# Four reciprocal norms reach all partitions through a row in DRAM instead of products with the identity

## The chip, the cores and the metric

The kernel runs as one program on one core of a Trainium2 chip. The metric is the device time of one execution in microseconds (us); the figures below are a median of three runs and one profiled execution. TensorE is called PE here, its weight loads PEld, VectorE DVE, ScalarE ACT, GpSimd POOL and the DMA queue of SyncE SP. A profile line number such as L289 is a line of the kernel file before the change.

## The reference

A trunk of two layers over 512 tokens of width 1024, all in float32. Each layer has a mixing part and a SwiGLU feed-forward part (FFN), and each part first divides every token by the root mean square of its 1024 features.

```python
def rms_norm(x, g):
    x32 = x.astype(jnp.float32)
    y = x32 * lax.rsqrt(jnp.mean(x32 * x32, axis=-1, keepdims=True) + EPS)
    return (y * g).astype(x.dtype)

def reference(x, ...):
    h = x
    for layer in range(DEPTH):                      # 2
        hn = rms_norm(h, mixer_norm_g[layer])
        if layer % 2 == 0:                          # retention and pooling, joined
            h = h + retention_pool_mixer(hn, positions, ...)
        else:                                       # pointwise + GLU, causal conv of width 31,
            h = h + conformer_conv(hn, ...)         # LayerNorm, swish, pointwise
        h = h + swiglu(rms_norm(h, ffn_norm_g[layer]), w_gate[layer], w_up[layer], w_down[layer])
    return rms_norm(h, final_norm_g)
```

So there are five such norms: one ahead of the mixer of layer 0, one ahead of each FFN, one ahead of the convolution part of layer 1, and the final one. The first four are touched by the change.

## The kernel before, in words

The residual `X` lies in SBUF feature-major: 128 features on the partitions, 8 tiles of features, 512 tokens along the free dimension. Products run in float32 accuracy as three products of split operands: a high part, rounded, and a low part that holds the rest (`mm3`: high by high, high by low, low by high). Weights come in chunks of 1 MB into a ring of two raw buffers (`wr`), and are split into a high part `wh` (ACT cast) and a low part `wl`. For most chunks `wl` is a DVE subtraction (L186); for the second and third chunk of each FFN and most chunks of the convolution part ACT writes minus the high part and a DMA issued by POOL adds the raw values to it (L178, L1353). A raw buffer is free for the next load only when that DMA has landed.

The norm is not applied to the operand: `X` times its gain goes into the products, and the reciprocal root `r` of each token multiplies their results. Since tokens lie along the free dimension of those results, `r` is needed as a tile with the same 512 values on every partition. The steps of one norm are:

- squares of `X` are summed over the feature tiles into `acc` [128 x 512];
- `token_sums` (L281) multiplies each block of 128 tokens of `acc`, as the stationary operand, by a column of ones. That gives a PSUM tile [128 x 4] with token `128 t + p` at partition `p`, column `t`;
- `inv_rms` (L296) scales it and `rsqrt` (L264 to L271) takes the reciprocal root with eleven small DVE instructions;
- `spread` (L284) takes each of the four columns, broadcast along the free dimension, as the stationary operand of a product with the identity, which puts the 128 values on every partition; ACT copies the PSUM tile to SBUF (L293).

Where it is done:

- In the mixer, `rtok` (the result of `rsqrt`) is also used per token as a column, for `v` (L614) and for the gate (L651). Its spread form multiplies the tables `cosr` and `sinr` of the rotary positions (L497, L498) and the channels of the pooling groups (L534), out of which ACT and DVE make the split operands `yh` and `yl` of the product `ps_p`.
- In each FFN the first three chunks of gate and up weights are ordinary products (`ps_gu`); the spread stands inside the second of these (between its k = 4 and k = 5, L987), and the DVE instruction L884 in `hidden` reads it first. The further 19 chunks go through `cycle`, a scheme with seven half products in place of eight.
- In the convolution part the spread stands inside the second projection `proj(1)` (L1381); `gated` (L1191) reads it for each of the eight projections. Between those DVE instructions DVE works through 31 taps of the depthwise convolution for each of three feature tiles (`some_taps`, L1329); PE does the other five tiles (`conv_tile`). After the taps of two tiles, `pivot_sum` adds them into `acc` (L1301), whose token sums PE forms.

Order: in the FFNs the order on PE, DVE and ACT is the program's (`manual_schedule`); SP and POOL are placed by a planner, which lists instructions by its own costs. In the convolution part SP is in program order too. In the mixer only the first block is in program order; from `rb = spread(rtok, "rms")` (L496) on, the planner places everything. In the convolution part a chunk's raw load is one `start_load()`, and `split_rest` is a generator whose two steps each cast half a chunk; its second step is run inside `gated`, after the sigmoid:

```python
                rest = split_rest()
                next(rest)
                proj(4)
                some_taps(1)
                gated(3, pss[3], FULL, two_taps, rest)
                to_rows(3, FULL)
                start_load()
                some_taps(9)
```

Of the kernel before, what the change touches and what calls it, by code (L numbers as in the profile page):

```python
# [10 lines left out]
F32 = mybir.dt.float32  # L11
# [3 lines left out]
ALU = mybir.AluOpType  # L15
PSUM = bass.MemoryType.PSUM

P = 128
D = 1024
S = 512  # L20
KT = D // P
NT = S // P
# [7 lines left out]
EPS = 1e-6  # L30
# [3 lines left out]
FULL = slice(0, S)  # L34
# [49 lines left out]
def trunk(ctx: ExitStack, tc: tile.TileContext, a: dict):  # L84
    nc = tc.nc
# [7 lines left out]
    wk = ctx.enter_context(tc.tile_pool(name="wk", bufs=2))  # L93
    pmm = ctx.enter_context(tc.tile_pool(name="pmm", bufs=3, space=PSUM))
    paux = ctx.enter_context(tc.tile_pool(name="paux", bufs=2, space=PSUM))

    vec = const.tile([P, NVEC], F32, name="vec")
    con = const.tile([P, NCON], F32, name="con")
# [13 lines left out]
    ones = C("ones")  # L112
# [90 lines left out]
    def feature_major(ps, wh, wl, xh, xl, cols=FULL, between={}, ks=range(KT)):  # L203

        for k in ks:
            if k in between:
                between[k]()
            for i in range(2):
                c = slice(i * P, (i + 1) * P)
                mm3(ps[:, i, cols], wh[:, k, c], wl[:, k, c], xh[k][:, cols], xl[k][:, cols], k == 0, k == KT - 1)  # L210
# [27 lines left out]
    xgh = [None] * KT  # L238
    xgl = [None] * KT
# [32 lines left out]
            between()  # L272
        return y

    def token_sums(acc, cols=FULL):

        ps = paux.tile([P, S], F32, tag="aux", name="ps_ms")
        n = (cols.stop - cols.start) // P
        for t in range(n):
            at = cols.start + t * P  # L280
            nc.tensor.matmul(ps[:, t:t + 1], lhsT=acc[:, at:at + P], rhs=ones, start=True, stop=True)  # L281
        return ps[:, :n]

    def spread(v, name, out=None):  # L284

        n = v.shape[1]
        ps = paux.tile([P, S], F32, tag="aux", name=f"ps_{name}")
        for t in range(n):
            nc.tensor.matmul(ps[:, t * P:(t + 1) * P], lhsT=v[:, t:t + 1].to_broadcast([P, P]),  # L289
                             rhs=ident, start=True, stop=True)  # L290
        if out is None:
            out = wk.tile([P, n * P], F32, tag=f"bc_{name}", name=f"bc_{name}", bufs=1)
        nc.scalar.copy(out, ps[:, :n * P])  # L293
        return out

    def inv_rms(acc):  # L296
        v = sm.tile([P, NT], F32, tag="ms", name="ms")
        nc.vector.tensor_scalar(v, token_sums(acc), 0.5 / D, 0.5 * EPS, ALU.mult, ALU.add)
        return rsqrt(v, NT, "a4")

    def new_acc():
# [26 lines left out]
    def mixer():  # L328
        with ExitStack() as m:
# [9 lines left out]
            acc = new_acc()  # L339
# [64 lines left out]
            with tc.manual_schedule(engines={mybir.EngineType.PE, mybir.EngineType.DVE, mybir.EngineType.Activation,  # L404
# [68 lines left out]
                ps = token_sums(acc)  # L473
# [4 lines left out]
                v = sm.tile([P, NT], F32, tag="ms", name="ms")  # L478
# [11 lines left out]
            for src in range(2):  # L490
                ps_, ts_ = slice(src * HP, (src + 1) * HP), slice(src * HS, (src + 1) * HS)
                for dst in range(2):
                    pd = slice(dst * HP, (dst + 1) * HP)
                    nc.scalar.activation(cosr[pd, ts_], kq[ps_], AF.Sin)
                    nc.scalar.activation(sinr[pd, ts_], ang[ps_], AF.Sin, scale=2.0 * dst - 1.0)
            rb = spread(rtok, "rms")  # L496
            nc.vector.tensor_tensor(cosr, cosr, rb, ALU.mult)  # L497
            nc.vector.tensor_tensor(sinr, sinr, rb, ALU.mult)  # L498

# [157 lines left out]
            acc = new_acc()  # L657
# [39 lines left out]
    def ffn_in(layer, acc, gain, fx, fl, fh, fe, ff):  # L697
# [275 lines left out]
        scaled(2)  # L973
        scaled(3)
        combined_lo(1)
        r = inv_rms(acc)
        load_gu(f0)
        plain_hi(f0)
        load = split_load()
# [4 lines left out]
        for _ in load:  # L984
            pass
        ps.append(pair("ps_gu1"))
        feature_major(ps[1], *w, xgh, xgl, between={5: lambda: row.update(rb=spread(r, "rms"))})  # L987
        add_up(f0)
        combined_lo(2)
        combined(3)  # L990
# [175 lines left out]
    def conv(acc):  # L1166
        with ExitStack() as m:
# [167 lines left out]
            def note(name, f, *args):  # L1335
                row[name] = f(*args)
# [22 lines left out]
            def proj(j, between={}):  # L1359
                pss[j] = pair(f"ps_pw{j}")  # L1360
                feature_major(pss[j], *chunk("w_pw1", j, 0), xgh, xgl, between=between)
# [10 lines left out]
            with tc.manual_schedule(engines={mybir.EngineType.PE, mybir.EngineType.DVE, mybir.EngineType.Activation,  # L1372
# [5 lines left out]
                proj(0, {7: lambda: note("r", inv_rms, acc)})  # L1378
                for _ in split_rest():
                    pass  # L1380
                proj(1, {2: lambda: note("rb", spread, row["r"], "rms")})  # L1381
                rb = row["rb"]
                start_load()
                gated(0, pss[0], FULL)
                some_taps(9)
# [220 lines left out]
```

## Time and profile before

| | |
|---|---|
| median of 3 runs | 1048.3 us (1048.09 to 1048.49) |
| profiled execution: its own time, its span | 1047.62 us, 1045.8 us |
| granted clock of TensorE | 0.998 |
| busy share of the span: PE, PEld, DVE, ACT, POOL | 99%, 87%, 81%, 49%, 3% |
| DMA traffic | 121.63 MB, mean 116 GB/s |
| products of `spread` for the four norms (L289, `ps_rms`) | 32 rows of PE, median 275 ns |
| copies of the four spread tiles (L293, `bc_rms`) | 4, median 568 ns |
| token sums (L281) on `acc` | 48 rows of PE, median 250 ns |

A busy row of PE overlaps the next one, since products are pipelined; what a product costs is better read from the distance between the starts of two rows. In a timeline row the columns are start, duration, engine, line, operation, tiles and shape; the bracket at the end gives the idle time of that engine just before the row and what ended it. In a row of waits, the numbers are the total, how many, and the longest. In a row of windows, they are the length of the window, then busy time and number of instructions of PE, PEld, DVE, ACT and POOL, then the granted clock, the DMA share and GB/s. Rows of DMA issues end with the size of one transfer and its median time from issue to landing.

### The profile page before, as it was taken

The numbers are of one execution on the slowest core, as the hardware profiler recorded it, in microseconds if no ns is written. First come the engines' busy times: TensorE is split into PE (matmuls) and PEld (weight loads), VectorE is DVE, ScalarE is ACT, GpSimd is POOL, SyncE is SP. The second block draws the span as 40 slices with busy tenths as digits, with TensorE's granted clock in tenths as the row PEclk, the third lists the DMA queues.
The fourth block names the chain that finished last, engine by engine and source line by source line (L and its number), as shares of the span: only waits on it lengthen the run. The fifth ranks groups of instructions, "written<-read, shape, count | busy, mean of one in ns | idle before, by whom it ended". The sixth has DMA issues, their size and how long they took to land.

```text
span 1045.8 us, 16517 instructions
## 1 busy us (share of the span) xinstructions
PE 1035.9 (99%) x6705; PEld 907.9 (87%) x6705; DVE 850.5 (81%) x1297; ACT 515.9 (49%) x881; POOL 32.5 (3%) x33
## 2 busy tenths in 40 slices
PE   9999999999999999999999999999999999999997
PEld 7878888899999999998888665988999999999987
DVE  7888735889988889997779797859999888899855
ACT  8543134765454545543444325656654455445434
POOL 0000000100000000001121100000000000000000
PEclk9999999999999999999999999999999999999999
DMA  8322122643323322333248996146233332323122
GB/s 300 132 81 81 41 81 88 184 136 116 111 92 104 119 91 92 122 118 125 81 94 188 222 189 149 59 139 174 72 121 121 102 121 76 112 96 122 41 81 81
DMA packets 38108, 121.63 MB, mean 116 GB/s; under 512 B 4112, under 2 KB 13328, under 8 KB 29584
## 3 DMA queue, kind: packets, MB, share of 16 engines
q1 hardware_dynamic: 34432, 107.99, 32.4%
q0 software_dynamic: 3456, 12.58, 6.3%
q8 instruction: 52, 0.85, 0.3%
q14 instruction: 24, 0.20, 0.1%
q10 hardware_dynamic: 144, 0.00, 0.0%
HBM read 100.36 MB, written 2.10 MB: 98 GB/s over the span
## 4 chain that ended last, share of the span: by engine, by line
PE 88%; DVE 6%; ACT 2%; DMA 2%; issue 1%; DVEq 0%; ACTq 0%
PE ps_x L854 19%; PE ps_y L854 10%; PE ps_dn L199 7%; PE ps_dn L200 7%; PE ps_dn L201 7%; PE ps_z L854 5%; PE ps_c L1229 2%; PE ps_gu L201 2%; PE ps_gu L199 2%; PE ps_gu L200 2%; PE ps_pw L199 2%; PE ps_pw L201 2%; PE ps_pw L200 2%; DMA wr<-in_w_pw 2%; PE ps_wo L201 1%; PE ps_wo L200 1%
## 5 line engine op out<-in xcount | busy, mean ns | idle before, releaser
L854 PE MATMUL ps_x<-th,w 128*128 128x256 f32 x608 | 115.9, 276 | 0.3 <-ACT sn L929 0.3
L765 DVE TENSOR_TENSOR wg<-wg 128x512 f32<-128x512 f32 x152 | 105.3, 693 | 5.1
L774 ACT CAST w<-wg 128x512 fp32r<-128x512 f32 x152 | 82.9, 618 | 37.3 <-PE ps_y L854 36.0
L854 PEld LDWEIGHTS ps_x<-th,w 128*128 128x128 f32 x608 | 97.2, 188 | 0.5 <-ACT sn L929 0.5
L779 DVE TENSOR_TENSOR w<-wg,w 128x2048 fp32r<-128x2048 f32 x38 | 87.1, 2291 | 10.5 <-ACT w L774 10.1
L854 PE MATMUL ps_x<-tl,w 128*128 128x256 f32 x304 | 83.9, 276 | 0.0
L311 DVE TENSOR_TENSOR X<-X,ps_dn 128x1024 f32<-128x1024 f32 x46 | 56.0, 1218 | 18.6 <-PE ps_dn L201 18.6
L183 ACT CAST w<-wr 128x2048 fp32r<-128x2048 f32 (+2 forms) x22 | 34.8, 1599 | 56.6 <-PE ps_g L573 21.8
L199 PE MATMUL ps_dn<-hh,dh0d 128*128 128x512 f32 x152 | 59.4, 391 | 0.0
L200 PE MATMUL ps_dn<-hl,dh0d 128*128 128x512 f32 x152 | 59.4, 391 | 0.0
L201 PE MATMUL ps_dn<-hh,dl0d 128*128 128x512 f32 x152 | 59.2, 390 | 0.1
L854 PE MATMUL ps_y<-th,w 128*128 128x256 f32 x304 | 57.9, 276 | 0.0
L854 PE MATMUL ps_y<-xgh,w 128*128 128x256 f32 x304 | 57.9, 276 | 0.0
L854 PEld LDWEIGHTS ps_x<-tl,w 128*128 128x128 f32 x304 | 57.1, 188 | 0.0
L939 ACT COPY sn<-ps_x 128x256 f32<-128x256 f32 x38 | 14.2, 374 | 85.9 <-PE ps_x L854 85.9
L200 PE MATMUL ps_dn<-hl,dh1d 128*128 128x512 f32 x144 | 56.2, 391 | 0.0
L199 PE MATMUL ps_dn<-hh,dh1d 128*128 128x512 f32 x144 | 56.2, 391 | 0.0
L201 PE MATMUL ps_dn<-hh,dl1d 128*128 128x512 f32 x144 | 56.0, 389 | 0.0
L854 PE MATMUL ps_x<-xgh,w 128*128 128x256 f32 x288 | 55.2, 277 | 0.0
L878 DVE TENSOR_TENSOR hl<-act,hh 128x512 fp32r<-128x512 f32 x44 | 30.5, 692 | 26.3 <-ACT hh L877 26.1
L877 ACT CAST hh<-act 128x512 fp32r<-128x512 f32 x44 | 27.3, 621 | 48.0 <-DVE act L872 44.0
L199 PE MATMUL ps_pw<-xgh,w 128*128 128x512 f32 x128 | 50.3, 393 | 0.0
(346 smaller groups left out, 3098.9 us busy)
## 6 DMA issues: line engine op xcount, KB each, us to landing
wg<-in_w_gu SPq DMA_DIRECT2D x38, 1024.0 KB, 4.9
dr<-in_w_dn SPq DMA_DIRECT2D x64, 256.0 KB, 2.9
w<-wr POOLq DMA_DIRECT2D x24, 512.0 KB, 5.3
wr<-in_w_pw SPq DMA_DIRECT2D x10, 1024.0 KB, 5.1
wr<-in_w_gu SPq DMA_DIRECT2D x6, 1024.0 KB, 4.9
dr<-in_w_dn SPq DMA_DIRECT2D x32, 192.0 KB, 2.5
wr<-in_w_o SPq DMA_DIRECT2D x4, 1024.0 KB, 4.9
R<-u SPq DMA_DIRECT2D x12, 270.0 KB, 14.6
```

The lines of the kernel that those rows point to most:

```text
L183: nc.scalar.copy(wh[:, s], raw[:, s])
L199: nc.tensor.matmul(out, lhsT=wh, rhs=xh, start=start, stop=False)
L200: nc.tensor.matmul(out, lhsT=wh, rhs=xl, start=False, stop=False)
L201: nc.tensor.matmul(out, lhsT=wl, rhs=xh, start=False, stop=stop)
L311: nc.vector.tensor_tensor(xx, xx, ps, sign)
L765: nc.vector.tensor_tensor(o, o, i, ALU.add)
L774: nc.scalar.copy(block(sums[f][0], *SUMS[i]), block(raw_g[f], *SUMS[i]))
L779: nc.vector.tensor_tensor(l, raw_g[f], h.bitcast(F32), ALU.subtract)
L854: nc.tensor.matmul(out, lhsT=u[:, k, :], rhs=v, start=first and k == 0 and n == 0, stop=k == 3 and n == 2, skip_group_check=True)
L877: nc.scalar.copy(hh[f], s)
L878: return lambda: nc.vector.tensor_tensor(hl[f], s, hh[f].bitcast(F32), ALU.subtract)
L1229: nc.tensor.matmul(ps[32 * i:32 * i + 32, :n], lhsT=dgs[j][:, i, g, :], rhs=Rs[j][:, i, 4 * g + cols.start:4 * g + cols.stop], start=g == ...
```

## The change

`spread` stays for the three uses inside the convolution part's LayerNorm. For the four norms `spread_row` takes its place: one DMA on SP writes the 512 values into a row of 2 KB in DRAM, a second DMA on SP reads that row back to all 128 partitions (256 KB in SBUF). For the two FFNs and the convolution part the token sums are formed with tokens taken in steps of four (`by=NT`), so that partition `p` holds the tokens `4p` to `4p + 3`, four neighbours of 16 bytes in the row. In the mixer `rtok` keeps its layout, as `v` and the gate use it; there the write puts single values 512 bytes apart. The result tile has the same name `bc_rms`. In the FFNs the call now stands directly behind `inv_rms`, in the convolution part ahead of `proj(1)`, in the mixer at the place of the old call.

```diff
+    dr = ctx.enter_context(tc.tile_pool(name="dr", bufs=2, space=bass.MemoryType.DRAM))
...
-    def token_sums(acc, cols=FULL):
+    def token_sums(acc, cols=FULL, by=1):
         ps = paux.tile([P, S], F32, tag="aux", name="ps_ms")
         n = (cols.stop - cols.start) // P
+        if by > 1:
+            for t in range(n):
+                nc.tensor.matmul(ps[:, t:t + 1], lhsT=acc.rearrange("p (q t) -> p t q", t=n)[:, t, :], rhs=ones,
+                                 start=True, stop=True)
+            return ps[:, :n]
...
+    def spread_row(v, name, tokens="(p t) -> p t"):
+        row = dr.tile([S], F32, tag="row", name=f"row_{name}")
+        out = wk.tile([P, S], F32, tag=f"bc_{name}", name=f"bc_{name}", bufs=1)
+        nc.sync.dma_start(row.rearrange(tokens, t=NT), v)
+        nc.sync.dma_start(out, row.partition_broadcast(P))
+        return out
+
     def inv_rms(acc):
         v = sm.tile([P, NT], F32, tag="ms", name="ms")
-        nc.vector.tensor_scalar(v, token_sums(acc), 0.5 / D, 0.5 * EPS, ALU.mult, ALU.add)
+        nc.vector.tensor_scalar(v, token_sums(acc, by=NT), 0.5 / D, 0.5 * EPS, ALU.mult, ALU.add)
         return rsqrt(v, NT, "a4")
...   (mixer)
-            rb = spread(rtok, "rms")
+            rb = spread_row(rtok, "rms", "(t p) -> p t")
...   (FFN)
-        r = inv_rms(acc)
+        row["rb"] = spread_row(inv_rms(acc), "rms")
         load_gu(f0)
         plain_hi(f0)
         load = split_load()
...
-        feature_major(ps[1], *w, xgh, xgl, between={5: lambda: row.update(rb=spread(r, "rms"))})
+        feature_major(ps[1], *w, xgh, xgl)
...   (convolution part)
-                proj(1, {2: lambda: note("rb", spread, row["r"], "rms")})
-                rb = row["rb"]
+                rb = spread_row(row["r"], "rms")
+                proj(1)
                 start_load()
```

## The prediction

> **What bounds the kernel now.** I read the totals first, then what the weight loads of TensorE (PEld) waited for, then the four places where the rows are spread, each as a timeline.
>
> ```profile
> span 1045.8 us, 16517 instructions
> PE 1035.9 (99%) x6705; PEld 907.9 (87%) x6705; DVE 850.5 (81%) x1297; ACT 515.9 (49%) x881; POOL 32.5 (3%) x33
> PEld ps_p L199 <- ACT yh L231: 1.3, 3, 0.5
> ...
> PEld ps_gu L201 <- DMA w<-wr: 0.7, 2, 0.4
> L289 PE MATMUL ps_rms<-con,rs_y x32: 271/275/275, 31.3 to 715.5; 128*128 128x128 f32 x32
> L281 PEld LDWEIGHTS ps_ms<-con,acc x48: 186/192/192, 24.2 to 707.6; 128*128 128x128 f32 x48
> ```
>
> PE is busy for 1035.9 of 1045.8 us, so whatever PE no longer does could come back one for one, unless PE then stands at one of its waits. Two of them are quoted (total, number, longest): in the mixer PE waits for yh, which ACT casts from pooled channels made on DVE; in the two FFN layers, once each, for the low part of a weight chunk, w<-wr, which POOL's accumulating DMA finishes. A third, in the convolution layer, comes below. The removed work is 32 rows on PE, 8 for each of the four norms (an f32 product shows as two).
>
> **Price of one spread on PE.** FFN of layer 0:
>
> ```profile
> 200.25 0.39 PE L200 MATMUL ps_gu<-xgl,w 128*128 128x512 f32 x1
> 200.47 0.39 PE L201 MATMUL ps_gu<-xgh,w 128*128 128x512 f32 x1
> ...
> 201.82 0.39 PE L200 MATMUL ps_gu<-xgl,w 128*128 128x512 f32 x1
> ```
>
> Products of 512 columns start 0.22 us apart (200.25, 200.47). Two of them after the one at 200.47 the row at 201.82 should have started at 200.92; it started 0.90 us later. One spread costs PE 0.9 us, four 3.6 us. That is the most that this part can give. The four ACT copies that go save nothing of their own: ACT is busy for half of the span, and where the copy does end a wait (the convolution layer) it is counted there.
>
> **Mixer: -0.9.**
>
> ```profile
> 29.89 0.16 DVE L271 SCALAR_TENSOR_TENSOR rs_y<-rs_t,rs_y 128x4 f32<-128x4 f32 x1
> 34.24 0.33 SPq L147 DMA_DIRECT2D wr<-in_w_u  x1
> 40.47 0.69 DVE L497 TENSOR_TENSOR cosr<-cosr,bc_rms 128x512 f32<-128x512 f32 x1 [3.88 <-ACT cosr L494]
> ```
>
> rtok is ready at 30.05 (29.89 + 0.16). DVE uses the spread row only at 40.47, where it waited for the cosines. A row that lands before that costs nothing: the two transfers have 10.4 us of cover, and the mixer's write, the slowest of the four, is priced among the rivals. Without that cover DVE, and through yh PE, would be late one for one. SP issues its next load at 34.24; if that has to pass the second transfer it shifts by at most the time of one write. PE's 0.9 us can come back here. What speaks against it is the wait for yh (1.3 us of weight loads, three times): DVE's chain from 40.47 does not move, so PE would reach yh sooner. But the order of PE's products there is the planner's, and others can stand in front. Bounds: 0 if those waits take it all, -0.9 if they take nothing; I take -0.9, since the waits are short and the products between them many.
>
> **The two FFN layers: 0 on PE, +0.2 each by traffic.**
>
> ```profile
> 181.09 0.33 SPq L720 DMA_DIRECT2D wg<-in_w_gu  x1
> 194.02 0.33 SPq L147 DMA_DIRECT2D wr<-in_w_gu  x1
> 197.99 0.16 DVE L271 SCALAR_TENSOR_TENSOR rs_y<-rs_t,rs_y 128x4 f32<-128x4 f32 x1
> 199.10 1.05 ACT L176 CAST w<-wr 128x1024 fp32r<-128x1024 f32 x1 [0.26 <-DMA wr<-in_w_gu]
> 201.53 0.86 POOL L178 DMA_DIRECT2D w<-wr  x1 [11.78 <-ACT w L177]
> w<-wr POOLq DMA_DIRECT2D x1, 512.0 KB, 4.6
> 206.16 0.49 PE L201 MATMUL ps_gu<-xgh,w 128*128 128x512 f32 x1
> 206.75 1.22 DVE L884 TENSOR_TENSOR gu<-ps_gu,bc_rms 128x1024 f32<-128x1024 f32 x1
> 209.59 3.80 SPq L720 DMA_DIRECT2D wg<-in_w_gu  x2
> 719.91 0.39 PE L200 MATMUL ps_gu<-xgl,w 128*128 128x512 f32 x1
> 720.29 0.50 PE L201 MATMUL ps_gu<-xgh,w 128*128 128x512 f32 x1
> ```
>
> The third chunk of weights is loaded by SP at 194.02, cast by ACT at 199.10 (it waited for that load), and its low part is accumulated by POOL at 201.53, landing 4.6 us later at 206.13. PE reads it at 206.16, 0.03 later. In layer 1 the same product shows the wait plainly: it starts at 720.29, 0.38 after the one at 719.91 instead of 0.22. This chain of SP, ACT and POOL starts before the spread and contains no product of it, so with 0.9 us less work PE stands 0.9 us longer at the same product. Gain 0, twice; a gain is excluded because PE already waits. The new token sums have the same 8 loads; a slower load would be hidden in this 0.9 us too. The row is needed at 206.75: r ends at 198.15 and two transfers have 8.6 us. Behind them on SP comes a load that is not issued before 209.59, so nothing else is late there. What can be lost is traffic: the 256 KB read runs from about 200.5 to 203.5, and w<-wr moves its 512 KB from about 202.4 on. Half a microsecond is the upper bound (dr below takes 0.9 longer for 256 KB than the shortest transfer; two that share take half of that from each other), 0 the lower; I take +0.2 each, nearer to 0, as the two overlap for one microsecond of three.
>
> **Convolution layer: +1.8.** This is where the change decides.
>
> ```profile
> 532.45 0.16 DVE L271 SCALAR_TENSOR_TENSOR rs_y<-rs_t,rs_y 128x4 f32<-128x4 f32 x1
> 536.44 1.23 DVE L1191 TENSOR_TENSOR gu<-ps_pw,bc_rms 128x1024 f32<-128x1024 f32 x1 [3.79 <-ACT bc_rms L293]
> 541.61 14.48 SPq L147 DMA_DIRECT2D wr<-in_w_pw  x2
> 536.00:538.00 2.00, 2.00 (x11) 1.63 (x10) 1.23 (x1) 1.97 (x3) 0.86 (x1) 1.00 1.10 207
> 539.27:578.76 39.49, 39.49 (x176) 32.69 (x175) 39.03 (x59) 17.04 (x18) 5.25 (x7) 1.00 0.80 187
> 570.61 0.86 POOL L1353 DMA_DIRECT2D w<-wr  x1 [1.98 <-ACT w L1352]
> w<-wr POOLq DMA_DIRECT2D x1, 512.0 KB, 9.2
> 579.91 0.34 SPq L147 DMA_DIRECT2D wr<-in_w_pw  x1
> 591.98 1.04 ACT L1351 CAST w<-wr 128x1024 fp32r<-128x1024 f32 x1 [10.97 <-DMA wr<-in_w_pw]
> 594.76 0.75 DVE L1196 SCALAR_TENSOR_TENSOR u<-gu,vec,act 128x512 f32<-128x512 f32 x1 [5.12 <-ACT act L1192]
> 605.45 1.05 PE L281 MATMUL ps_ms<-con,acc 128*128 128x1 f32 x8 [0.29 <-DVE acc L1301]
> ```
>
> r is there at 532.61. Before, the products and the copy brought it to DVE at 536.44, and DVE stood idle for 3.79 us. From then on DVE is full: 39.03 of 39.49 us up to 578.76. Out of that queue comes gated(3), behind whose sigmoid ACT casts half a chunk, which POOL accumulates at 570.61 (9.2 us to landing, 579.81); this frees the buffer for SP's load at 579.91, ACT's cast waits for that load until 591.98 with the sigmoid of gated(5) behind it, DVE waits 5.12 us for the sigmoid, does 14 more taps, and PE waits for the sum at 605.45. So a late row goes through DVE, ACT, POOL, SP, a DMA, ACT and DVE to PE without a gap larger than the 0.46 us that DVE had free. PE's own 0.9 us is lost at 605.45, where it waits already.
>
> How late is the row? Both transfers are on SP, the second behind the completion of the first. Nothing else is held up on SP: its next load is issued at 541.61, for a buffer that is not free before. No row shows a small write to DRAM; the nearest are these:
>
> ```profile
> DMA to landing us min/median/max: 2.0/2.5/2.7
> dr<-in_w_dn SPq DMA_DIRECT2D x64, 256.0 KB, 2.9
> vg<-in_vec ACTq DMA_DIRECT2D x1, 4.0 KB, 3.1
> R<-u SPq DMA_DIRECT2D x4, 142.0 KB, 3.9
> ```
>
> The first is out<-o, the only writes to DRAM in the trace (256 KB): 2.0 at least, 2.5 in the median. vg, 128 short runs, took 3.1. For the write of 128 runs of 16 B I take 2.25, bounds 2.0 and 3.1. For the 256 KB read, dr took 2.9 for the same size; the DMA engines are full at that time (share 1.10 in 536 to 538, POOL's accumulations), so 3.2, bounds 2.5 (the median of out<-o) and 3.9 (R<-u, which moves half as much in 512 runs). With 0.1 us ahead of each issue: 532.61 + 2.25 + 3.2 + 0.2 = 538.26, which is 1.8 us after 536.44. Bounds: 537.3 (+0.9) and 539.8 (+3.4). I do not subtract DVE's free 0.46 us: the read will hold up POOL's accumulations about as much.
>
> [...]
>
> **The sum**: -0.9 (mixer) + 0.2 + 0.2 (FFN) + 1.8 (convolution) = +1.3 us. The profiled execution took 1047.62 us, so 1048.9; it lies 0.7 below the median of the runs, 1048.3, which becomes 1049.6.
>
> **Rivals.**
> All of PE's time comes back: 1048.3 - 3.6 = 1044.7. This is the case on the faster side. It needs the row in the convolution layer by 536.44, both transfers in 3.8 us, where the shortest write alone took 2.0, and w<-wr in the FFNs 0.9 us sooner, which nothing in the change brings. Against it stand both waits above. 7 in 100.
> SP's order: SP is outside the manual order in the FFN, and the planner places the two transfers. If they come ahead of the load at 194.02, that load waits for r, the write and its own turn: 198.15 + 2.25 + 0.5 (0.33 to issue the read, as in the row at 194.02, and 0.2 ahead of two issues) = 200.9, 6.9 us late, and PE with it, in two layers: +13.8 - 0.9 + 1.8 gives 1063. For it: a list order by program text has them first. Against: SP's wg at 181.09 was issued ahead of the dr loads of the same layer, which stand before it in the program, so the plan goes by what is ready, and r is 4 us behind the load. 10 in 100.
> Strided weight loads: token sums now read every fourth element, 16 B apart. The same loads now, from contiguous columns, take 186 to 192 ns (L281 above). If the 8 products go from 1.05 us (row at 605.45) to twice that, r of the convolution layer is 1.0 later: 1050.6. [...] 10 in 100.
> Mixer's row late: its write is 512 runs of 4 B, as rtok keeps its layout. R<-u with as many runs took 3.9, which gives 30.05 + 3.9 + 2.9 + 0.2 = 37.1, 3.4 us in hand; beyond 40.47 it delays DVE one for one. At 2 us late: 1051.6. 8 in 100.
> The late row is absorbed in the convolution layer, by a shorter transfer than the 9.2 and 12 us: only -0.9 + 0.4 remain, 1047.8. 5 in 100.
>
> **Numbers.** My sum has 60 in 100; its own range is 1048.3 (-0.9 + 0 + 0.9) to 1052.7 (0 + 1.0 + 3.4). 0.2% is 2.1 us, about what a measurement of this kernel can tell from no change: below 1046.2 and above 1050.4. Of my 60, 42 lie within and 18 above; the first rival and a small rest (8) are faster; absorbed (5) and part of the strided and mixer cases (5) are within, SP's order and the rest of those two above. Taken together 0.08, 0.52, 0.40. The range 1047.0 to 1053.0 reaches below to the absorbed case without the FFN's 0.4 (1047.4) and 0.4 of scatter (the runs shown lie 0.4 apart), above to the end of my own range and 0.3, and leaves out the first two rivals and little else.
>
> **What would show it.** Right: no L289 row for ps_rms; PE's wait for w<-wr in each FFN about 0.9 us longer; DVE's L1191 some 5.6 us instead of 3.8 after its r; PE's wait for acc of L1301 near 3 us. Wrong: the load of the third chunk behind the row's read on SP; weight loads of ps_ms longer than 192 ns; DVE's L497 waiting for the row instead of the cosines; the two transfers done within 4 us.

## The result, and the profile after

The changed kernel takes 1059.4 us (median of 4 executions, 1057.5 to 1059.6) against 1048.2 for the kernel before in the same runs: ratio 1.0104, 95% interval 1.0086 to 1.0121, 11.2 us slower. The prediction was 1049.6, its range 1047.0 to 1053.0. Line numbers of the changed file are larger: `token_sums` L282 (strided) and L287, `spread_row` L307 (write) and L308 (read), the mixer's first use L512, the convolution layer's first use L1206. One disturbed execution each of two kernels below (c4 1297.5 us, k1 5982) is left out of the times. A ratio is worked out from all executions of both kernels, so it is not the quotient of the two medians. The kernel before scatters too: in the sessions of the experiments its medians were 1047.8 to 1048.1, and 9 of its 92 executions took 1050.2 to 1052.8.

Totals of the page after, then from the view of waits what TensorE (PE) waited for (total, times, longest):

```profile
span 1057.8 us, 16454 instructions
PE 1040.3 (98%) x6673; PEld 910.3 (86%) x6673; DVE 850.2 (80%) x1297; ACT 513.9 (49%) x877; POOL 32.5 (3%) x33
```

```profile
PE ps_u L200 <- DVE qk L526: 4.6, 1, 4.6
PE ps_pw L202 <- DMA w<-wr: 2.0, 2, 1.5
PE ps_ms L287 <- DVE acc L1316: 1.4, 1, 1.4
```

PE is busy 4.4 us longer although 32 rows are gone from it. That is already a sign that the same products ran slower somewhere. The wait on ps_u is new.

Where the 12 us lie is read from loads that SP issues in both kernels. After:

```profile
187.25 0.33 SPq L735 DMA_DIRECT2D wg<-in_w_gu  x1
...
522.71 0.33 SPq L148 DMA_DIRECT2D wr<-in_w_pw  x1
...
701.47 0.33 SPq L735 DMA_DIRECT2D wg<-in_w_gu  x1
```

Before, the first of these stood at 181.09 (shown in the prediction), the other two here:

```profile
516.69 0.33 SPq L147 DMA_DIRECT2D wr<-in_w_pw  x1
...
689.63 0.33 SPq L720 DMA_DIRECT2D wg<-in_w_gu  x1
```

The shift is 6.16 at the first load of FFN 0, 6.02 at the convolution layer's, 11.84 at FFN 1's, 12.0 at the end. So the mixer lost 6.2 us, the convolution layer 5.8, the two FFNs nothing.

**Mixer.** From the timelines of SP, DVE and PE:

```profile
30.14 0.38 SPq L307 DMA_DIRECT2D row_rms<-rs_y  x1
38.26 0.34 SPq L308 DMA_DIRECT2D bc_rms<-row_rms  x1
38.69 0.38 SPq L148 DMA_DIRECT2D wr<-in_w_u  x1
44.52 0.69 DVE L512 TENSOR_TENSOR cosr<-cosr,bc_rms 128x512 f32<-128x512 f32 x1 [7.86 <-DMA bc_rms<-row_rms]
54.68 0.80 PE L200 MATMUL ps_u<-xgh,w 128*128 128x512 f32 x1 [4.56 <-DVE qk L526]
55.28 0.63 PE L201 MATMUL ps_u<-xgl,w 128*128 128x512 f32 x1
55.70 0.63 PE L202 MATMUL ps_u<-xgh,w 128*128 128x512 f32 x1
```

DVE stood 7.86 us for the row, the end of that wait being 4.05 us later than the 40.47 of before, and PE stood 4.56 us ahead of ps_u, whose PSUM buffer DVE frees when it has turned qk (the rotary step, L526). At yh, the wait that the prediction named, PE did not stand. Behind ps_u's first product, products start 0.43 us apart (55.28, 55.70) instead of 0.22. The view of windows (length, busy time of PE, PEld, DVE, ACT and POOL with the number of instructions, granted clock, DMA share, GB/s) shows it, and where the time of the write went:

```profile
31.00:31.50 0.50, 0.50 (x4) 0.42 (x3) 0.47 (x2) 0.24 (x1) 0.00 (x0) 1.00 0.51 4
31.50:38.00 6.50, 6.50 (x31) 5.37 (x30) 4.61 (x8) 2.44 (x4) 0.00 (x0) 1.00 0.00 0
55.00:60.00 5.00, 5.00 (x13) 3.85 (x13) 4.57 (x6) 3.64 (x5) 0.00 (x0) 0.50 0.03 11
```

From 55 to 60 the granted clock was 0.50. From 31.5 to 38.0 the DMA engines moved nothing at all: the 512 single values had left by 31.5, and SP was told of their completion only at 38.2. Of the issues near that place and near the convolution layer's row (size, us from issue to landing), in this order the mixer's write, the convolution layer's write and read:

```profile
row_rms<-rs_y SPq DMA_DIRECT2D x1, 2.0 KB, 8.1
...
row_rms<-rs_y SPq DMA_DIRECT2D x1, 2.0 KB, 1.4
...
bc_rms<-row_rms SPq DMA_DIRECT2D x1, 256.0 KB, 3.8
```

The sum for the mixer: -0.9 (no spread on PE) + 4.56 (PE idle) + some 2.6 (half of the 5.3 us from 54.7 to 60 at half clock) = 6.3, measured 6.2.

**Convolution layer.** The weight loads of the token sums, contiguous and strided (min, median, max in ns), then the rows around the norm in the timeline, and one of windows:

```profile
L287 PEld LDWEIGHTS ps_ms<-con,acc x24: 187/192/193, 24.3 to 667.2; 128*128 128x128 f32 x24
L282 PEld LDWEIGHTS ps_ms<-con,acc x24: 308/330/332, 198.9 to 720.2; 128*128 128x128 f32 x24
```

```profile
535.20 2.03 PE L282 MATMUL ps_ms<-con,acc 128*128 128x1 f32 x8 [0.23 <-DVE acc L257]
...
539.63 0.33 SPq L307 DMA_DIRECT2D row_rms<-rs_y  x1
...
544.90 1.23 DVE L1206 TENSOR_TENSOR gu<-ps_pw,bc_rms 128x1024 f32<-128x1024 f32 x1 [5.26 <-DMA bc_rms<-row_rms]
```

```profile
538.00:541.00 3.00, 3.00 (x9) 2.33 (x8) 1.36 (x10) 1.74 (x2) 0.00 (x0) 0.51 0.03 1
```

A strided load takes 330 ns instead of 192, the 8 products 2.03 us instead of 1.05, so r is 1.0 later. DVE gets the row at 544.90; before it was at 536.44, with the shift of 6.02 at 542.46: 2.4 us late. And for 3.4 us behind the sums (538.04 to 541.44 by windows of 1 us) PE ran at half clock, 9 products in 3 us. By the starts of the same products in both profiles PE was then 1.65 us late: 1.0 by the slow sums and 1.6 by half clock, less the 0.9 of the spread. The late DVE comes on top. Weight loads then waited three times, 3.4 us in all, for w<-wr, the low part that POOL accumulates (before, none did), which put PE back by 3.0, and PE stood 1.4 us instead of 0.3 for acc. This makes 5.7 of the 5.8 at the end of the layer.

### The profile page after: what moved, and what is told of

The parts are those of the page before. It is cut to its first block, busy times and chain, and to the rows that moved or that the text cites. A ratio compares the mean times of both kernels' runs of the same rounds, so it can differ in the third digit from the quotient of the medians.

```text
span 1057.8 us, 16454 instructions
## 1 busy us (share of the span) xinstructions
PE 1040.3 (98%) x6673; PEld 910.3 (86%) x6673; DVE 850.2 (80%) x1297; ACT 513.9 (49%) x877; POOL 32.5 (3%) x33
## 4 chain that ended last, share of the span: by engine, by line
PE 87%; DVE 4%; DMA 4%; ACT 2%; issue 1%; POOL 0%; DVEq 0%; ACTq 0%; SPq 0%; POOLq 0%
PE ps_x L869 19%; PE ps_y L869 10%; PE ps_dn L201 7%; PE ps_dn L200 7%; PE ps_dn L202 7%; PE ps_z L869 5%; PE ps_c L1244 2%; PE ps_gu L202 2%; PE ps_gu L200 2%; PE ps_gu L201 2%; DMA wr<-in_w_pw 2%; PE ps_pw L200 1%; PE ps_pw L201 1%; PE ps_pw L202 1%; PE ps_wo L202 1%; PE ps_wo L201 1%
## 5 line engine op out<-in xcount | busy, mean ns | idle before, releaser
L202 PE MATMUL ps_pw<-xgh,w 128*128 128x512 f32 x128 | 50.9, 398 | 2.1 <-DMA w<-wr 2.0
L200 PE MATMUL ps_pw<-xgh,w 128*128 128x512 f32 x128 | 50.8, 397 | 0.0
```

The costliest lines, as they stand in the source:

```text
L200: nc.tensor.matmul(out, lhsT=wh, rhs=xh, start=start, stop=False)
L202: nc.tensor.matmul(out, lhsT=wl, rhs=xh, start=False, stop=stop)
```

## The experiments

**Undoing one place at a time.** e1: the mixer's spread by products again. e2: the convolution layer's spread by products, its sums contiguous. e3: both. e4: the mixer's row alone, but turned first.

```diff
e1  -            rb = spread_row(rtok, "rms", "(t p) -> p t")
    +            rb = spread(rtok, "rms")
e2  -                rb = spread_row(row["r"], "rms")
    -                proj(1)
    +                proj(1, {2: lambda: note("rb", spread, row["r"], "rms")})      # and inv_rms(acc) with by=1
e4  -            rb = spread_row(rtok, "rms", "(t p) -> p t")
    +            nc.tensor.matmul(pt[:NT, :P], lhsT=rtok, rhs=ident, start=True, stop=True)
    +            nc.scalar.copy(rT, pt[:NT, :P])
    +            rb = spread_row(rT, "rms", None)         # row written as "(t p) -> t p": 4 runs of 512 B
```

> The changed kernel with the mixer's spread by products again; FFNs and convolution layer keep the row. Theory: the mixer's late row costs 6.2 of the 11.2 us, by stretches of the two profiles, so the time is 1059.4 - 6.2 = 1053.2 (1052.5 to 1054), 1.0048 of before; DVE's first use of bc_rms in the mixer waits for ACT's cosines again, PE has no idle time on ps_u and no stretch at half clock. Rival, the loss in the mixer merely moves: products and copy bring 0.9 us back to PE and the later parts take up the rest, the time stays above 1056.

> The changed kernel with the convolution layer's spread by products again, its token sums from contiguous columns; mixer and FFNs keep the row. Theory: the convolution layer costs 5.8 us of its own, so 1059.4 - 5.8 = 1053.6 (1053 to 1054.5). Rival, the convolution layer only suffers from what lies ahead of it (a later start, another order of transfers): then it stays late and the time is above 1057.

> Mixer and convolution layer as before, only the two FFNs take the row. Theory: PE's saved 0.9 us each is lost at the wait for w<-wr and in the slower strided weight loads (330 against 190 ns, 8 of them, some 1.0 us), so 1048.2 within 0.7. Rival A, PE's work comes back: 1048.2 - 1.8 = 1046.4. Rival B, the traffic of the row or the strided loads delay w<-wr: 1048.7 to 1050.

> FFNs and convolution layer as before. The mixer takes the row, but rtok is first turned on PE by one product with the identity (4 x 128 instead of 8 rows of spread), copied by ACT, and written as 4 runs of 512 B in place of 512 single values. Theory, the scattered write makes the row late: write and read take about 1.4 + 4 to 6 us, the row is there at 38 to 40, DVE waits for the cosines as before (40.5), no idle time on ps_u: 1048.2 - 0.7 to 1048.2 + 0.3. Rival, any trip through DRAM with the loads of w_u beside it is too slow or holds up the loads: row after 40.5 and the time above 1049.5, with PE idle ahead of ps_u.

| | median us (range, executions) | ratio to before, 95% |
|---|---|---|
| e1, rows in FFNs and convolution layer | 1051.7 (1049.8 to 1056.8, 10) | 1.0044 (1.0025 to 1.0062) |
| e2, rows in mixer and FFNs | 1055.2 (1053.4 to 1057.0, 4) | 1.0063 (1.0046 to 1.0081) |
| e3, rows in FFNs | 1048.3 (1047.4 to 1049.1, 11) | 1.0001 (0.9992 to 1.0010) |
| e4, turned row in the mixer | 1047.4 (1047.1 to 1050.8, 11) | 0.9995 (0.9986 to 1.0004) |

The two losses add up: 0.44% and 0.63% against 1.04% for both. The medians of e1 and e2 both miss the forecast range, e1 by 0.8 below and e2 by 0.7 above; single executions of e1 lie 7 us apart. The FFNs cost and bring nothing. A row through DRAM is not too slow for the mixer as such. In e4 the timeline of SP shows the write at 32.34 and the read behind its completion 1.2 us later, and DVE waits for the cosines as before; then DVE's step that frees a buffer of ps_qk, and PE's first product in it, in e4 and, last, before:

```profile
32.34 0.33 SPq L307 DMA_DIRECT2D row_rms<-rT  x1
33.53 0.35 SPq L308 DMA_DIRECT2D bc_rms<-row_rms  x1
...
40.71 0.69 DVE L516 TENSOR_TENSOR cosr<-cosr,bc_rms 128x512 f32<-128x512 f32 x1 [3.88 <-ACT cosr L509]
...
50.14 0.68 DVE L530 TENSOR_TENSOR qk<-ps_qk,cosr 128x512 f32<-128x512 f32 x1
50.88 0.50 PE L200 MATMUL ps_u<-xgh,w 128*128 128x512 f32 x1
```

```profile
50.82 0.39 PE L199 MATMUL ps_u<-xgh,w 128*128 128x512 f32 x1
```

But a gain cannot be told from nothing either. PE starts ps_u at 50.88, 0.06 after DVE is done with qk (50.82), and no earlier than before, so at least a part of what the row saves on PE is waited away at that buffer.

**The mixer's write.** Is it the scattered write or SP, which in the change holds the load of w_u behind the read? m2 issues both transfers from POOL. m4 splits the write into four of 128 values. In both, the other places are as before.

```diff
m2  -        nc.sync.dma_start(row.rearrange(tokens, t=NT), v)
    -        nc.sync.dma_start(out, row.partition_broadcast(P))
    +        nc.gpsimd.dma_start(row.rearrange(tokens, t=NT), v)
    +        nc.gpsimd.dma_start(out, row.partition_broadcast(P))
m4  -        nc.sync.dma_start(row.rearrange(tokens, t=NT), v)
    +        for t in range(NT):
    +            nc.sync.dma_start(row.rearrange("(t p) -> p t", t=NT)[:, t:t + 1], v[:, t:t + 1])
```

> FFNs and convolution layer as before; the mixer's row is written in 512 single values as in the change, but both transfers are issued by POOL, so SP's load of w_u is issued at about 34.3 us again and not behind the row. Theory: the scattered write takes 6 to 8 us on any queue, the row is at 42 to 45 us, later than 40.5, DVE is late by 2 to 4.5 us, PE stands ahead of ps_u and runs at half clock after it: 1047.8 + 3 to 7. Rival: the loss came from SP, the held load and its sharing with the read: the row is there by 41 us and the time is within 0.7 of before.

> FFNs and convolution layer as before; the mixer's row of 512 single values is written by four transfers of 128 values, one behind the other on SP (0.4 us apart). Theory (the completion of a scattered write takes time for each value): each lands after about a quarter of 8.1 us, the last by 34 to 35, the row before 41, time within 1 us of before. Rival (any write of single values has a long completion, some 6 us behind its last packet): the last lands at 37 to 39, the read behind it and behind the load of w_u, the row after 44, time +5 or more.

m2: 1055.7 us (1055.5 to 1055.9, 4), ratio 1.0073 (1.0057 to 1.0088). m4: 1055.0 us (1054.5 to 1055.6, 4), ratio 1.0065 (1.0047 to 1.0083). For m2 the row of its write among the DMA issues and DVE's first use of the row in the timeline; for m4 the timeline of SP and DVE and the row of its writes:

```profile
row_rms<-rs_y POOLq DMA_DIRECT2D x1, 2.0 KB, 11.4
```

```profile
46.84 0.69 DVE L512 TENSOR_TENSOR cosr<-cosr,bc_rms 128x512 f32<-128x512 f32 x1 [9.54 <-DMA bc_rms<-row_rms]
```

```profile
34.26 0.33 SPq L148 DMA_DIRECT2D wr<-in_w_u  x1
40.89 0.32 SPq L309 DMA_DIRECT2D bc_rms<-row_rms  x1
...
46.01 0.69 DVE L513 TENSOR_TENSOR cosr<-cosr,bc_rms 128x512 f32<-128x512 f32 x1 [9.40 <-DMA bc_rms<-row_rms]
```

```profile
row_rms<-rs_y SPq DMA_DIRECT2D x4, 0.5 KB, 9.0
```

In m4 the load of w_u is issued at 34.26, as early as before (34.24), and the row is late all the same, its read issued once the last write has landed: the held load is not the cause. Nor does the time shrink with the number of values behind one completion: the four writes of 128 values land after 9.0 us in the median, one of 512 after 8.1, and from POOL's queue after 11.4. Against that, 128 runs of 16 B took 1.4 us in the changed kernel (2.7 once, in an FFN of e2) and, at the same place in the mixer, 4 runs of 512 B 1.2. So it is the single values of 4 B; a write of 128 such values with no other beside it was not run. What the memory does in that time no view shows. The expectation of a quarter of 8.1 was wrong; that of m2 had the direction, but its +7.9 and its row at 46.84 lie beyond the forecast +7 and 45.

**The convolution layer: lateness, sums or traffic?** c1 has the row there alone, with contiguous sums: the last addition of squares writes the tokens regrouped. c2 is the kernel before with DVE held up, no row. c3 is the kernel before with strided sums, no row. c4 has the row there alone, with strided sums, as the change has it.

```diff
c1  -            nc.vector.tensor_tensor(acc, acc, sq, ALU.add)                # k = 7 only
    +            nc.vector.tensor_tensor(acct.rearrange("p (t q) -> p q t", t=NT),
    +                                    *[x.rearrange("p (q t) -> p q t", t=NT) for x in (acc, sq)], ALU.add)    # and token_sums(acct)
c2  +                nc.vector.memset(late, 0.0)                               # 128 x 4
    +                for _ in range(33):
    +                    nc.vector.tensor_tensor(late, late, late, ALU.mult)
                     gated(0, pss[0], FULL)
c3  +                nc.tensor.matmul(ps[:, t:t + 1], lhsT=acc.rearrange("p (q t) -> p t q", t=n)[:, t, :], rhs=ones, ...
    -        nc.scalar.copy(out, ps[:, :n * P])
    +        nc.scalar.copy(out.rearrange("p (q t) -> p t q", t=n), ps.rearrange("p (t q) -> p t q", t=n))
```

> Only the convolution layer takes the row. Its last addition of squares writes the sums of squares with the tokens regrouped, so that the token sums load contiguous columns and still put tokens 4p to 4p + 3 on partition p. In the version with the row in FFNs and convolution layer the executions lay between 1049.8 and 1056.8, and the changed kernel's profile shows TensorE at half clock for 3.4 us right behind the strided token sums (2.03 us for 8 products, 1.05 before). Theory A: the stretched sums trip the clock, at random; with contiguous loads the row is 1.0 us earlier, DVE 1.4 to 1.9 us late, no half clock, and the time is 1047.8 + 1.4 to 2.0 in nearly all executions. Theory B: the late row alone opens gaps on PE that trip the clock: the executions spread as before, over 5 us or more. Rival C, the DRAM traffic: also unchanged.

> The kernel before, with 34 small DVE instructions of some 0.197 us ahead of the first gated step in the convolution layer: DVE starts it at about r + 6.7 us, as late as with the row (some 2.8 us later than before), with no row, no traffic and contiguous token sums. Theory A (lateness costs its own size, the rest is the clock tripped by strided sums): 1047.8 + 2.4 to 2.9, narrow spread, mean clock as before. Theory B (lateness opens gaps that trip the clock): spread from +2 to +9. Rival C (the loss comes from the row's transfers on SP and the DMA engines, not from DVE): below +1.

> The kernel before, but the convolution layer's token sums load every fourth column; the spread stays on PE and the ACT copy puts the tokens back in order. No row. Theory A (strided sums stretch PE's thin stretch to some 2.5 us and trip the clock in part of the executions): DVE 1.0 us late, time +1.0 in the good executions, +2.5 to +5 in the others, wide spread. Theory B: +1.0 to +1.3, as narrow as before.

> Only the convolution layer takes the row, as the change has it (strided token sums); mixer and FFNs as before. It differs from the version whose sums load contiguous columns (median 1050.5, no execution above 1051.9) in the strided loads alone. Theory A (lateness gives some +2 to +3, and the strided sums of 2.03 us trip TensorE's clock to half for 3.4 us in part of the executions, after which DVE's and PE's delays add): median 1051 to 1053, some executions at 1053 to 1057, lower mean clock in those. Theory B (the wide spread of the version with the row in FFNs and convolution layer came from the FFN of layer 1 or from chance): all executions between 1049.5 and 1052.

| | DVE's gated(0), profiled, us late | median us (range, executions) | ratio to before, 95% |
|---|---|---|---|
| c1 | 2.0 | 1050.5 (1049.4 to 1051.8, 11) | 1.0025 (1.0016 to 1.0034) |
| c2 | 2.7 | 1051.0 (1050.1 to 1051.8, 7) | 1.0025 (1.0015 to 1.0036) |
| c3 | 2.6 | 1051.5 (1049.8 to 1052.1, 6) | 1.0031 (1.0019 to 1.0043) |
| c4 | 2.3 | 1051.7 (1050.0 to 1053.7, 11) | 1.0024 (1.0012 to 1.0036) |

Late is measured against 536.44, less the shift of the layer's first load. c2 loses as much as the kernels with the row, without any transfer: DVE's lateness is enough for the loss, and rival C, which needs a loss below 1, falls. (c2 still has the spread's 0.9 us on PE, so a small part for the transfers in c1 and c4 is not excluded.) c3's DVE was 2.6 us late where 1.0 was meant, which I put down to its strided copy, an estimate; with no row it loses the same. c1 and c4 differ in the strided loads alone and cannot be told apart by their ratios, though only c4 has executions above 1052. For c2 and then c3, one row of PE's timeline and one of windows:

```profile
579.10 0.50 PE L201 MATMUL ps_pw<-xgh,w 128*128 128x512 f32 x1 [2.23 <-DMA w<-wr]
```

```profile
581.00:583.00 2.00, 2.00 (x6) 1.61 (x5) 2.00 (x4) 1.87 (x2) 0.00 (x0) 0.50 1.03 247
```

```profile
529.25 2.03 PE L281 MATMUL ps_ms<-con,acc 128*128 128x1 f32 x8 [0.28 <-DVE acc L256]
```

```profile
532.00:534.00 2.00, 2.00 (x6) 1.53 (x5) 1.42 (x10) 0.40 (x1) 0.00 (x0) 0.50 0.00 0
```

Both theories hold a part. In c3 half clock follows the strided sums, in c2 it follows a wait of 2.23 us for a weight chunk that came late. In c2 products start 0.43 us apart from 580.13 to 583.54, so for 3.4 us; in c4 half clock lasts as long by windows of 1 us, from 532.54 to 535.94. Where the clock was whole in the layer (c1 and e1, both profiled at a mean clock of 0.999), loss and lateness agree by the marks of the profile: c1 lost 1.9 us with DVE 2.0 late, e1 2.8 with 2.8. With one event the loss is larger than the lateness: 4.4 against 2.7 in c2, 3.5 against 2.6 in c3, 2.9 against 2.3 in c4. So c1's forecast of +1.4 to 2.0 was too low, and c2's, a clock as before, did not hold in the profiled execution. PE lost the time mostly at w<-wr (2.0 us in c1, 2.2 in c2, 1.2 in c4), and at most 0.5 at the sums behind the taps (acc). But none of these four reaches the 1056 of e1.

**With the FFNs' rows.** r2 is e1 again, r1 the same with contiguous sums in all three places, on the same chip.

```diff
r1  -        nc.vector.tensor_scalar(v, token_sums(acc, by=NT), 0.5 / D, 0.5 * EPS, ALU.mult, ALU.add)
    +        nc.vector.tensor_scalar(v, token_sums(acct), 0.5 / D, 0.5 * EPS, ALU.mult, ALU.add)   # acct as in c1
```

> Rows in both FFNs and the convolution layer as in the change, the mixer as before, but the token sums of all three load contiguous columns (the last addition of squares regroups the tokens). Theory A: half clock behind the strided sums adds 1 to 5 us at random; without it the loss of the convolution layer is its lateness, +1.4 to +2.8, the FFNs give 0, so a median of 1049.5 to 1050.8 and no execution above 1053. Theory B: the lateness alone makes the wide spread: a median of 1051 to 1052 with a third or more of the executions above 1054, as beside it in the same version with strided loads.

> The version with rows in FFNs and convolution layer and strided sums once more, beside the one with contiguous sums. Both theories: a median near 1051.7, between 1049.8 and 1056.8. Theory A: lower mean clock (0.996 or less) in the executions above 1053, and, if the profiled one is among them, PE products 0.43 us apart right behind the strided sums or behind a later wait.

r1: 1052.3 us (1048.4 to 1054.8, 10), ratio 1.0034 (1.0019 to 1.0050). r2: 1056.0 us (1051.9 to 1057.4, 6), ratio 1.0065 (1.0044 to 1.0085). r2's profiled execution is one of the long ones. It loses 9.2 us in the convolution layer; PE's timeline and two windows:

```profile
529.66 2.03 PE L282 MATMUL ps_ms<-con,acc 128*128 128x1 f32 x8 [0.23 <-DVE acc L257]
...
613.47 1.10 PE L287 MATMUL ps_ms<-con,acc 128*128 128x1 f32 x8 [4.39 <-DVE acc L1316]
```

```profile
533.00:535.00 2.00, 2.00 (x6) 1.52 (x5) 0.93 (x7) 1.21 (x2) 0.00 (x0) 0.50 0.02 1
615.00:617.00 2.00, 2.00 (x12) 0.39 (x8) 2.00 (x3) 0.92 (x2) 0.00 (x0) 0.50 1.03 266
```

Half clock twice: behind the sums, and once more behind the wait of 4.39 us for DVE's acc, which was 0.3 before. I read it so: the first slows PE, that and the late row make DVE late, DVE makes PE wait, and the wait brings half clock again; the links between were not tested one by one. In r1's profile the layer lost 2.7 us, with DVE 2.2 late, and the clock was whole in it. So the strided loads are worth about 3.7 us here by the two medians and 3.2 by the ratios; the two intervals overlap a little, so the size is uncertain. Without them r1 still spreads over 6 us: theory A is right in direction, but its median and its "no execution above 1053" are wrong, and theory B's third above 1054 is one of ten. r2's median lies 4.3 above the forecast. The forecast on the clock came true: in e1 and r2 together, the eight executions above 1053 have a mean clock of 0.993 to 0.996, the other eight 0.997 to 0.999. Why c1 and c4, without the FFNs' rows, spread less than r1 and r2 stays open.

**When the clock falls.** The windows in which r2's two stretches at half clock begin show some order in what looks like chance:

```profile
532.00:533.00 1.00, 1.00 (x5) 0.80 (x4) 0.83 (x6) 0.00 (x0) 0.00 (x0) 0.71 0.00 0
...
614.00:615.00 1.00, 1.00 (x9) 0.69 (x12) 0.42 (x4) 0.00 (x0) 0.22 (x1) 0.67 0.51 140
```

Between a clock of 1.00 and one of 0.50, a mean of 0.71 puts the beginning at 532.42, one of 0.67 at 614.34: 81.92 us apart, 24 times 3.413. By windows of 1 us half clock begins at 53.34, 538.04 and 1053.44 in the changed kernel, at 532.54 and 1044.54 in c4, at 55.42 and 1048.70 in m4, at 532.42, 614.34 and 1051.24 in r2, the last of each at the kernel's end. Within each profile these beginnings lie whole multiples of the same 3.413 us (a 24th of 81.92) apart, to 0.02, and the stretches inside the kernel last one such length (3.40 and 3.42 us) or, in the mixer, two (6.82 in the changed kernel, 6.84 in m4). The 3.41 us ahead of a beginning hold the wait and the strided sums of the convolution layer whole: 534.97 to 537.23 in the changed kernel, 529.36 to 531.64 in c4, 529.43 to 531.69 in r2, and 528.97 to 531.28 in c3, where half clock begins between 531.68 and 532.00. In e1, with the same sums, the clock stays whole (1.00 from 530 to 534); why, no view shows. The FFNs' strided sums, 1.80 us without a wait, are followed by a whole clock in the changed kernel (1.00 in the windows from 200 to 204 and from 720 to 724); steps of 3.413 us counted from 538.04 fall within them, at 200.12 and 718.95. So in these profiles 2.2 us or more of waiting and one-column products came before half clock, though not in e1, and 1.8 did not; where the limit lies was not shown.

**The FFNs' 0.9 us.** f1: the kernel before, with the low terms of the third chunk's product last. f2: the same, and both FFNs take the row with contiguous sums. k1: f2 and e4's mixer.

```diff
f1  -        feature_major(ps[2], *w, xgh, xgl)
    +        for low in range(2):                         # 32 products with wh first, then 16 with wl
    +            for k in range(KT):
    +                for i in range(2): ...
```

> The kernel before, with one change of order in both FFNs: in the third chunk's product all terms with the low part of the weights come after the 32 terms with the high part, so PE needs the low part that POOL accumulates some 7 us later. Theory: PE waits there for w<-wr only 0.2 to 0.4 us in each layer, so 1047.9 - 0 to 0.6. Rival: PE's next wait (for DVE's or ACT's operands of the first cycle) takes up the rest: no change.

> As the kernel with the low terms last, and the two FFNs take the row, with token sums from contiguous columns (the last addition of squares regroups the tokens). Theory: the 0.9 us of each spread was lost because PE waited for w<-wr and the strided loads took 1.0 us; with both out of the way it comes back: 1.8 us below the kernel with the low terms last, about 1046 (1045.5 to 1046.8). Rival: PE then stands at the next operand (DVE's sums for the first cycle) and the gain is below 0.5 us.

> The parts that cost nothing, together: the mixer with rtok turned by one product and written as 4 runs of 512 B, both FFNs with the row, contiguous token sums and the low terms last, the convolution layer as before. By the sum of the parts: -0.4 (mixer, measured -0.05% with an interval of 0.09%) and -1.8 (FFNs) = 1045.7 (1045 to 1047), if the FFN theory holds; 1047.5 if it does not.

| | median us (range, executions) | ratio to before, 95% |
|---|---|---|
| f1 | 1047.8 (1047.0 to 1051.7, 12) | 0.9996 (0.9985 to 1.0006) |
| f2 | 1045.7 (1044.8 to 1046.5, 8) | 0.9971 (0.9959 to 0.9983) |
| k1 | 1045.9 (1044.6 to 1050.8, 11) | 0.9980 (0.9967 to 0.9993) |

PE's wait in e3, then the second mark of FFN 0 (its fourth load of this kind) in e3 and in f2; the first mark stood at 181.13 and 181.26:

```profile
PE ps_gu L202 <- DMA w<-wr: 1.2, 1, 1.2
```

```profile
231.12 0.33 SPq L735 DMA_DIRECT2D wg<-in_w_gu  x1
```

```profile
230.06 0.33 SPq L742 DMA_DIRECT2D wg<-in_w_gu  x1
```

From first to last mark FFN 0 takes 49.85 us before, 49.73 in f1, 49.99 in e3 and 48.80 in f2; FFN 1 55.46 before and 54.24 in f2. In e3 FFN 1 takes 56.54, and PE's wait of 1.2 is there: the row brings nothing, and the profiled execution even loses 1.1 us in that layer. Moving that wait away alone (f1) brings nothing that can be told from no change either. Nor do contiguous sums alone: in r1, which has the row and the contiguous sums but not f1's order, the FFNs take 49.98 and 55.59. All three together bring 1.1 and 1.2 us, somewhat more than the 0.9 of one spread. Row and f1's order with strided sums was not run. f2 is faster than the kernel before by 0.29%, and so than f1 and e3. k1 should have been better still by the mixer's part and is not: the two cannot be told apart.

## Why the prediction was wrong, and where it was right

**Mixer (-0.9, measured +6.2).** The failed step is the price of the write in the rival "mixer's row late". The row was put at 37.1, from R<-u, which has as many runs and took 3.9; the write took 8.1, and the read, with the load of w_u issued 0.43 us behind it, 6.2 instead of 2.9: 4.2 and 3.3 us too little, against 3.4 in hand. R<-u was the wrong neighbour, and misread: by the code (`to_rows`) each of these transfers has 128 runs of 284 values, 512 only in the four together, and they go to SBUF. The rival's rule, beyond 40.47 one for one, was also too low: 4.05 us late gave 6.2, because PE, 0.9 earlier, stood 4.56 us and then worked at half clock. Whether the -0.9 can be had at all stays open: in e4, with the row in time, PE waits at ps_u's buffer, and e4's 0.9995 cannot be told from no change. By windows of 1 us the clock was halved here from 53.34 to 60.16, that is from 3.2 us into PE's wait, which ran from 50.12 to 54.68. In c2 half clock stood behind a wait of 2.23 us. The prediction had no clock in it at all.

Of the 8.1 us of the mixer's write 6.7 lie behind its last packet, by the windows from 31.5 to 38.0. The write of 16 B runs took 1.4 us in all, below the 2.0 that the prediction had as its lower bound.

**FFNs (0 on PE, measured 0).** Right in the number, and in part in its reason. In the changed kernel the wait for w<-wr did not grow: its weight loads waited 0.7 us as before, and PE did not stand there. Nearly all of the 0.9 went into the strided sums, 1.80 us for 8 products in FFN 0 instead of 0.95, which the prediction had thought hidden in that wait:

```profile
PEld ps_gu L202 <- DMA w<-wr: 0.7, 2, 0.4
```

```profile
199.11 1.80 PE L282 MATMUL ps_ms<-con,acc 128*128 128x1 f32 x8
```

Behind the sums stands the wait that the prediction meant: f2 shows that the gain is there once both are out of the way. The +0.2 each for traffic cannot be told from nothing: e3 lies at 1.0001, with PE's wait of 1.2 in one profiled layer and none in the other. The forecast that this wait grows by 0.9 is seen only where the sums are contiguous and nothing else takes the time, in r1's waits:

```profile
PE ps_gu L202 <- DMA w<-wr: 1.9, 2, 1.0
```

Before, its 0.7 us were a matter of weight loads alone; here PE itself stands 1.9 us.

**Convolution layer (+1.8, measured +5.8; 1.9 to 9.2 in the other profiles with the row there).** That a late row makes DVE late, and that lateness PE's loss, was right: c2 gives the same loss by lateness alone. But the path was thought to end at PE's wait for acc; PE lost more at w<-wr, the low part that POOL accumulates on the way, 2.0 us in the changed kernel against 1.4 at acc. The terms: the write took 1.4 (2.25 taken), the read 3.8 (3.2 taken), r came 1.0 later by the strided loads, a rival that was given 10 in 100 and is real (330 ns against 192). DVE was 2.4 us late in place of 1.8. What failed is the step from late to loss. My sum took lateness one for one, which held, nearly, only in the profiles with a whole clock in the layer (lost and late: c1 1.9 and 2.0, e1 2.8 and 2.8, r1 2.7 and 2.2), and the strided rival priced the sums' second effect, half clock behind them, at nothing. What c2, c3 and r2 show was not in it: half clock behind a wait of 2.23 us (c2) or behind 2.03 us of one-column products (c3, r2), for 3.4 us in c2 and r2, and in r2 perhaps the next wait by it.

The rival "SP's order" did not come about: in the FFNs both transfers stand behind the load of the third chunk. Nor did "all of PE's time comes back". Of the signs named for being wrong, two came: weight loads of 330 ns, and DVE in the mixer waiting for the row instead of the cosines.

## What to carry to other kernels

Where the busiest engine is TensorE, price a late operand as lateness plus what the clock takes: in the changed kernel's convolution layer 0.23 us of waiting and 2.03 us of one-column products had 3.4 us at half clock behind them, some 1.6 us of loss; in e1's profile the clock stayed whole. Before a vector goes through DRAM, bring it into runs: its write took 1.4 us in runs of 16 B and 1.2 in runs of 512 B, 8.1 in single values; turning it took one product on TensorE (e4). And removed work gains only once the next wait in line is moved too: f1 and e3 alone bring nothing; together, with contiguous sums (f2), 0.29%.

## What was not expected of the hardware

A write of single 4 B values to DRAM completed 8.1 us after its issue with 512 values (11.4 from POOL's queue) and 9.0 us after it, in the median of four, with 128 values; in the changed kernel its packets were gone after 1.4 us. 128 runs of 16 B completed after 1.4 us in the changed kernel, 4 runs of 512 B after 1.2 in e4. A weight load with a step of 16 B took 330 ns instead of 192. TensorE's clock was at half not only behind waits of 2.23 us and more: 0.23 to 0.28 us of waiting and 2.03 us of one-column products came before it in the profiles of the changed kernel, c3, c4 and r2 (3.4 us long in the changed kernel, c4 and r2), while it stayed at 1.00 behind the sums in e1. The beginnings of half clock lie whole multiples of 3.413 us apart within each of the profiles of the changed kernel, c4, m4 and r2. What sets half clock off no view shows.
